# Latents and context laid out with features on partitions by the host; norm factors applied there, without transposes ahead of the projections

## The chip, the cores and the metric

The kernel runs on one core of a Trainium2 chip. The metric is the device time of one execution in microseconds (us); less is better. TensorE (PE in the profile) multiplies matrices; VectorE (DVE), ScalarE (ACT) and GpSimd (POOL) do the elementwise work; SyncE (SP) issues nearly all DMAs. PEld is the load of a matmul's stationary operand.

## The reference, cut to what matters here

One layer of a diffusion backbone: 512 latent tokens and 256 context tokens of 1024 features. The part that the change touches is the first norm, its modulation, and the first two groups of projection columns (384 for the latent queries, 256 for the latent keys and values):

```python
def rms_norm(x, g):
    y = x * lax.rsqrt(jnp.mean(x * x, axis=-1, keepdims=True) + EPS)
    return y * g
...
mod = jax.nn.silu(c) @ w_ada[layer] + b_ada[layer]
sh1, sc1, gt1, sh2, sc2, gt2 = jnp.split(mod[:, None, :], 6, axis=-1)
h  = rms_norm(x_lat, norm1_g) * (1 + sc1) + sh1
hc = rms_norm(x_ctx, norm1_g) * (1 + sc1c) + sh1c
...
q_c, kv_c, ... = split_columns(h @ w_in)
q_cc, kv_cc, ... = split_columns(hc @ w_in)
```

Behind it come latent attention, gated linear attention, a merge of both, and a gated MLP with a 3x3 convolution.

## The kernel before

A product in fp32 accuracy is made of three matmuls in the faster fp32r type: every operand is split into a high part (a cast) and a low part (operand less high part), and `mm3` multiplies high by high, high by low and low by high. The split of weights is a cast on ACT and a subtraction on POOL (`split`); that of the modulated tokens was two DVE instructions.

The features are cut into eight blocks of 128, j = 0 to 7. For each block, the projection loop (lines 553 to 679) needs three things:

- the modulation: the block's columns of `w_ada` (`load_ada`, two tiles of 512 KB) times `silu(c)` and `silu(c_ctx)`. `modulation(j)` makes 16 small matmuls and copies the result to SBUF (`rows`); `factors(j, rows)` turns it by one matmul with `sel` and leaves `shc` (shift) and `scc` (scale times norm gain) of the block, one number for each feature, that is for each partition;
- the block of tokens with features on partitions. The host gives tokens on partitions, so `squared` (sum of squares of a token on ACT), `rstd_exp` (reciprocal root) and `normalised` (DVE, in place) work there, then `columns` turns four 128x128 squares on PE into PSUM, `modulated` scales and shifts them on ACT, and casts and subtracts on DVE;
- the block's weights: `load_w`, `split_latents`.

Then `kv_latents(j)` makes six matmuls of 128x512 and `q_latents(j)` nine, all accumulating in PSUM over the blocks. Step j of the loop does the modulation of block n = j+1, the key-value products of block j, the factors of block n, the query products of block j, and between them starts the tokens of block n. Blocks of the context are turned in j = 5, 6 and 7; their products come behind the loop (`ctx_latents`).

Ahead of the loop, block 0 is done in two halves of 256 tokens: the first needs only the first two tiles of `x`. `fill` issues matmuls whose result is not used; eight stand at the very start, three behind the first factors.

In this stage PE, DVE, ACT, POOL and SP all keep the order in which the code is written (`pinned`), each engine in its own queue; behind the loop more and more of the order is set by a scheduler that works on a model of the time. DMAs count on eight semaphores in turn, so an issue waits for the transfer eight places ahead of it. Tiles come from pools: `raw` (3 buffers, the second half of `w_ada`'s blocks), `kT` (4, the weights), `P` (4, rows and modulated tokens), `s` (30 of 128x1024, most others). `split_wq(0)` splits the first block of `w_uq`, which is used behind the loop.

After the loop `totals` and `spread` serve two more norms: `spread` turns a column of 128 numbers into a 128x128 square with equal columns, by a matmul of the broadcast column with the identity.

Of the kernel before, what the change touches and what calls it, by code (L numbers as in the profile page):

```python
# [18 lines left out]
D = 1024  # L19
# [52 lines left out]
def block_kernel(ctx: ExitStack, tc: tile.TileContext, p, out):  # L72
# [276 lines left out]
    with tc.tile_pool(name="e1", bufs=1) as e1:  # L349
# [29 lines left out]

        def load_wq(k):  # L380
            wq_raw.append(EK())
            SY.dma_start(out=wq_raw[k], in_=w_uq[:, k, :])
# [9 lines left out]
        def split_latents(j, parts=(0, 1)):  # L392
            r = wraw[j]
            if j % 2 == 0 and 0 in parts:
# [3 lines left out]
            for i in parts:  # L398
                (h_, l_), w = both[i]
                if len(parts) == 1 and i == 1:  # L400
                    V.tensor_copy(h_, w)
                    sub(G, l_, w, f(h_))
                else:
                    split(h_, l_, w)
# [4 lines left out]
        def split_wq(k):  # L409
# [63 lines left out]
        def squared(t0):  # L473

            ss = sm(2, "ssx2")
            for t in range(2):
                A.activation(junk, xs[t0 + t], AF.Square, accum_out=ss[:, t:t + 1])
            return ss

        def normalised(t, a, b):  # L480

            V.tensor_scalar(out=xs[t][:, a:b], in0=xs[t][:, a:b], scalar1=rx[t // 2][:, t % 2:t % 2 + 1], scalar2=None,
                            op0=ALU.mult)

        rx = [None, None, None]

# [25 lines left out]
        tps = [0]  # L512

        def columns(j, ctx_, t0, n):

            tps[0] += not ctx_
            tp = (mp if j < 4 else single[j // 2 - 1])[:, j % 2 * 256:j % 2 * 256 + 256] if ctx_ else single[1 + tps[0] % 2]
            for t in range(n):
                PE.transpose(tp[:, t * 128:(t + 1) * 128], xs[4 * ctx_ + t0 + t][:, j * 128:(j + 1) * 128], ident)
            return tp  # L520

        def modulated(j, ctx_, t0, n, tp):
            ht = EP()
            if (j, ctx_, t0) == (0, 0, 0):
                V.tensor_scalar(out=ht[:, 0:128 * n], in0=tp[:, 0:128 * n], scalar1=scc[:, 0, 0:1],
                                scalar2=shc[:, 0, 0:1], op0=ALU.mult, op1=ALU.add)
            else:
# [27 lines left out]
        load_x(0)  # L555
        A.dma_start(out=cst[:, 0:132], in_=p["consts"][:, 0:132])
        load_x(1)
        load_ada(0)
        load_x(2)
        load_w(0, 384, 640)  # L560
        load_x(3)
        load_w(0, 0, 384)
# [3 lines left out]
        fill(accK, 8)  # L566
# [12 lines left out]
        ss = squared(0)  # L579
        rx[0] = rstd_exp(ss, 2, 1.0 / D)  # L580
        for t in range(2):
            normalised(t, 0, 256)
        rows = modulation(0)
        tp = columns(0, 0, 0, 2)
        factors(0, rows)
        fill(accK, 3)
        ss = sm(2, "ssx2")
        A.activation(junk, xs[2], AF.Square, accum_out=ss[:, 0:1])
        modulated(0, 0, 0, 2, tp)
        split_latents(0, [0])  # L590
        split_latents(0, [1])
        A.activation(junk, xs[3], AF.Square, accum_out=ss[:, 1:2])
        kv_latents(0, 0, 256)
        q_latents(0, 0, 256)
        rx[1] = rstd_exp(ss, 2, 1.0 / D)
# [1186 lines left out]
```

## Time and profile before

| | |
|---|---|
| median of 3 runs | 877.91 us (877.88 to 878.12) |
| profiled execution | 878.03 us |
| its span, first to last instruction | 876.3 us |
| granted TensorE clock, mean | 0.999 |
| first projection matmul (block 0, key-value) | 12.71 us |
| factor product of block 2 / 6 | 22.54 / 43.87 us |
| first key-value matmul of block 7 | 53.49 us |
| DMA moved in the span | 130.79 MB |

Times inside an execution count from the span's first instruction. In the rows of the timeline, the first number is the start, the second the length of the group; then the engine, the line (nearly all are L89, the line of the helper that issues every instruction), the operation, what it writes and reads (by tile names, buffer numbers left out), its shape and how many of it stand in the group, and in brackets how long the engine was idle before and what ended that. A matmul in plain fp32 appears as two records; an fp32r matmul and a transpose appear as one. `p` and `pb` are PSUM tiles, `cst` holds the identity.

### The profile page before, as it was taken

Reading aid. Unit: us, or ns where it says so; the run is one execution under the profiler, and the core shown is the slowest. Engines: PE = TensorE matmul, PEld = TensorE weight load, DVE = VectorE, ACT = ScalarE, POOL = GpSimd, SP = SyncE. Lnnn points to the kernel's source line nnn. Section 1 sums busy time; section 2 is a strip of 40 time slices with the busy share of each in tenths; the row PEclk is TensorE's granted clock in tenths of the full one; section 3 lists DMA queues with packets and bytes.
Section 4 is the critical chain, followed back from the end, with each engine's and each line's share of the span. In section 5 each row is a group of like instructions: output and inputs, shape, how many; then the busy total and the mean of one; then the engine's idle time right before and its main releaser. Section 6 shows DMA issues by size and latency. Waiting matters only on the chain.

```text
span 876.3 us, 12667 instructions
## 1 busy us (share of the span) xinstructions
PE 864.8 (99%) x4741; PEld 734.7 (84%) x4741; DVE 641.2 (73%) x1040; ACT 415.7 (47%) x671; POOL 374.6 (43%) x248
## 2 busy tenths in 40 slices
PE   8999999999999999999999999999999999999996
PEld 6888899888888888888888889888888888888885
DVE  6487788875978786985776665777776677677866
ACT  4366676773454545444545324433334334456415
POOL 3302364450534242534561404877767676400004
PEclk9999999999999999999999999999999999999999
DMA  9920001215313342535872512655536656386602
GB/s 357 380 77 1 1 6 32 74 49 193 108 37 132 109 132 61 176 101 210 306 288 85 180 49 73 221 194 206 199 124 231 218 193 194 100 300 221 225 30 97
DMA packets 41360, 130.79 MB, mean 149 GB/s; under 512 B 4785, under 2 KB 5313, under 8 KB 41298
## 3 DMA queue, kind: packets, MB, share of 16 engines
q1 hardware_dynamic: 40098, 126.87, 42.0%
q10 hardware_dynamic: 1008, 2.49, 0.7%
q8 instruction: 37, 0.61, 0.3%
q0 software_dynamic: 192, 0.63, 0.2%
q14 instruction: 25, 0.20, 0.1%
HBM read 116.13 MB, written 13.63 MB: 148 GB/s over the span
## 4 chain that ended last, share of the span: by engine, by line
PE 94%; DVE 3%; ACT 1%; issue 1%; POOL 1%; ACTq 0%; POOLq 0%
PE pb L89 50%; PE p L89 23%; PE pb L88 15%; PE p L88 6%; DVE s L89 1%; DVE mx L89 1%; DVE kT L89 0%; ACT P L89 0%; DVE P L89 0%; ACT s L89 0%; ACT kT L89 0%; POOL wlo L89 0%; DVE X L89 0%; DVE pl L89 0%; POOL s L89 0%
## 5 line engine op out<-in xcount | busy, mean ns | idle before, releaser
L89 POOL TENSOR_TENSOR wlo<-raw,whi 128x1024 fp32r<-128x1024 f32 (+1 forms) x93 | 213.0, 2298 | 254.7 <-ACT whi L89 221.1
L89 PE MATMUL pb<-s,whi 128*128 128x512 f32 (+1 forms) x874 | 269.5, 389 | 0.0
L89 PEld LDWEIGHTS pb<-s,whi 128*128 128x128 f32 x874 | 163.3, 188 | 33.5
L89 ACT CAST whi<-raw 128x1024 fp32r<-128x1024 f32 (+1 forms) x108 | 105.3, 977 | 159.3 <-PE pb L89 75.6
L89 PE MATMUL pb<-s,wlo 128*128 128x512 f32 (+1 forms) x437 | 169.9, 389 | 0.0
L89 DVE SCALAR_TENSOR_TENSOR ac<-pb,cwT,ac 128x441 f32<-128x441 f32 (+2 forms) x160 | 111.0, 694 | 23.4 <-ACT ac L89 18.9
L88 PE MATMUL pb<-s,whi 128*128 128x512 f32 x320 | 101.2, 394 | 0.0
L89 PEld LDWEIGHTS pb<-s,wlo 128*128 128x128 f32 x437 | 82.0, 188 | 17.0
L89 PE MATMUL p<-s,s 128*128 128x512 f32 (+1 forms) x302 | 72.2, 390 | 0.6 <-DVE s L89 0.6
L88 PEld LDWEIGHTS pb<-s,whi 128*128 128x128 f32 x320 | 59.3, 188 | 11.5
L89 PEld LDWEIGHTS p<-s,s 128*128 128x128 f32 x302 | 55.4, 188 | 13.4 <-issue 1.9
L88 PE MATMUL pb<-s,wlo 128*128 128x512 f32 x160 | 62.8, 392 | 0.0
L89 PE MATMUL p<-whi,s 128*128 128x512 f32 x168 | 56.3, 393 | 0.0
L89 PE MATMUL pb<-whi,s 128*128 128x512 f32 x164 | 53.5, 390 | 0.0
L89 POOL TENSOR_TENSOR s<-s,edge 128x512 f32<-128x512 f32 x7 | 10.4, 1503 | 93.7 <-ACT s L89 93.7
L89 PE MATMUL p<-s,whi 128*128 128x256 f32 (+1 forms) x220 | 50.2, 322 | 0.0
L89 PE MATMUL pb<-s,s 128*32 128x128 f32 (+2 forms) x340 | 46.1, 319 | 0.0
L89 DVE TENSOR_TENSOR pl<-pb,ph 128x512 fp32r<-128x512 f32 x48 | 32.9, 686 | 13.3 <-ACT ph L89 12.8
L89 PE MATMUL p<-kT,s 128*128 128x512 f32 (+1 forms) x192 | 41.2, 350 | 0.9 <-ACT P L89 0.9
L89 PEld LDWEIGHTS pb<-s,s 128*128 128x128 f32 (+1 forms) x340 | 36.1, 159 | 5.8 <-issue 0.7
L89 ACT CAST ph<-pb 128x512 fp32r<-128x512 f32 x48 | 28.2, 587 | 20.9 <-PE pb L89 20.8
L89 PEld LDWEIGHTS p<-s,whi 128*128 128x128 f32 x220 | 35.7, 191 | 2.2
(269 smaller groups left out, 1655.6 us busy)
## 6 DMA issues: line engine op xcount, KB each, us to landing
raw<-in_up_dram SPq DMA_DIRECT2D x44, 512.0 KB, 4.2
rawd<-in_w_down_dram SPq DMA_DIRECT2D x22, 512.0 KB, 5.1
ws<-rawd SPq DMA_DIRECT2D x18, 512.0 KB, 5.4
s<-in_ada_rest_dram SPq DMA_DIRECT2D x12, 512.0 KB, 5.4
xn<-in_ada_rest_dram SPq DMA_DIRECT2D x10, 512.0 KB, 4.6
s<-in_ada_first_dram SPq DMA_DIRECT2D x8, 512.0 KB, 9.0
raw<-in_ada_first_dram SPq DMA_DIRECT2D x8, 512.0 KB, 8.1
raw<-in_in_ga_dram SPq DMA_DIRECT2D x8, 512.0 KB, 3.5
```

The source lines that it names most:

```text
L88: return fn(*args, **kw)
L89: ins = fn(*args, **kw)
```

## The change

The host adds `x_t`, the latents with features on partitions (four tiles, each with two blocks of 512 tokens), and `ctx_t` (two tiles, each with four blocks of 256). The kernel loads `x_t` in place of `x` at the start, and `ctx_t` besides `ctx`.

- The sums of squares of the latents: ACT squares three tiles and half of the fourth, DVE the other half; DVE adds the two blocks of a tile; `norm_sums` adds over partitions by matmuls with a column of ones, 16 in all. `spread_norm` turns the four columns of reciprocal roots into a 128x512 tile in PSUM, `spread_[0]`, by four transposes of a broadcast column. It stays there for all blocks.
- `modulated_in` replaces `columns`, `normalised` and `modulated`: `scaled_` (DVE) multiplies the block by `scc` and by the spread factors, `high` (ACT) adds the shift and rounds to the high part, `low` (DVE) adds the shift and subtracts the high part. `tiles` issues these three stages for several blocks side by side.
- The context keeps its squares on tokens (`x`'s layout, on ACT at j = 2); its spread factors follow at j = 4, and its blocks are modulated at j = 4 to 7.
- Block 0's queries are done over 512 tokens at once; its key-value products keep two halves. Modulation 7 is issued one step earlier.
- `fill` is 5 at the start and then single ones of 128 columns.
- `split_wq(0)` comes at j = 5 in place of 6, with its subtractions on POOL. `spread` uses transposes. In the merge loop (line 1386) a part of the gate moves from j = 6 to j = 5.

```diff
+        def load_xt(i):
+            xT[i] = S4f()
+            SY.dma_start(out=xT[i], in_=p["x_t"][i])
...
-                sub(V, l3[:, :, a:b], r3[:, :, c:c + b - a], f(h3[:, :, a:b]))
+                sub(V if k else G, l3[:, :, a:b], r3[:, :, c:c + b - a], f(h3[:, :, a:b]))
...
-        def columns(j, ctx_, t0, n):
-
-            tps[0] += not ctx_
-            tp = (mp if j < 4 else single[j // 2 - 1])[:, j % 2 * 256:j % 2 * 256 + 256] if ctx_ else single[1 + tps[0] % 2]
+        spread_ = [single[1], single[2]]
+
+        def spread_norm(dst, r_, n):
+
             for t in range(n):
-                PE.transpose(tp[:, t * 128:(t + 1) * 128], xs[4 * ctx_ + t0 + t][:, j * 128:(j + 1) * 128], ident)
-            return tp
-
-        def modulated(j, ctx_, t0, n, tp):
-            ht = EP()
...
-                A.activation(ht[:, 0:128 * n], tp[:, 0:128 * n], AF.Identity, scale=scc[:, j, ctx_:ctx_ + 1],
-                             bias=shc[:, j, ctx_:ctx_ + 1])
-            h_, l_ = cxt(j) if ctx_ else lat(j, t0 * 128, n * 128)
-            V.tensor_copy(h_, ht[:, 0:128 * n])
-            sub(V, l_, ht[:, 0:128 * n], f(h_))
+                PE.transpose(dst[:, t * 128:t * 128 + 128], r_[:, t:t + 1].broadcast_to([128, 128]), ident)
+
+        def norm_sums(sq, first, last):
+
+            for t in range(4):
+                mm(single[2][:, t:t + 1], sq[:, t * 128:t * 128 + 128], ones[:, 0:1], first and t == 0, last and t == 3)
+
+        def modulated_in(j, ctx_, a=0, b=512):
+            b = (b, 256)[ctx_]
+            ht = EP()[:, 0:b - a]
+            x_ = cT[j // 4][:, j % 4 * 256:j % 4 * 256 + 256] if ctx_ else xT[j // 2][:, j % 2 * 512 + a:j % 2 * 512 + b]
+            shift = shc[:, j, ctx_:ctx_ + 1]
+            h_, l_ = (cxt if ctx_ else lat)(j, a, b - a)
+
+            def scaled_():
+                V.scalar_tensor_tensor(out=ht, in0=x_, scalar=scc[:, j, ctx_:ctx_ + 1], in1=spread_[ctx_][:, a:b],
+                                       op0=ALU.mult, op1=ALU.mult)
+
+            def high():
+                A.activation(h_, ht, AF.Identity, bias=shift)
+
+            def low():
+                V.scalar_tensor_tensor(out=l_, in0=ht, scalar=shift, in1=f(h_), op0=ALU.add, op1=ALU.subtract)
...
-        load_x(0)
+        for i in range(4):
+            load_xt(i)
...
-        fill(accK, 8)
+        fill(accK, 5)
...
+        a_, b_ = slice(0, 512), slice(512, 1024)
+        for i in range(4):
+            sq = S4f()
+            if i < 3:
+                A.activation(sq, xT[i], AF.Square)
+            else:
+                A.activation(sq[:, a_], xT[i][:, a_], AF.Square)
+                tt(V, sq[:, b_], xT[i][:, b_], xT[i][:, b_], ALU.mult)
+            tt(V, sq[:, a_], sq[:, a_], sq[:, b_], ALU.add)
+            norm_sums(sq, i == 0, i == 3)
+            if i < 2:
+                fill(accK, 1, 128)
+        rx = rstd_exp(single[2][:, 0:4], 4, 1.0 / D)
         rows = modulation(0)
-        tp = columns(0, 0, 0, 2)
         factors(0, rows)
-        fill(accK, 3)
...
+        fill(accK, 1, 128)
+        spread_norm(spread_[0], rx, 4)
+        fill(accK, 1, 128)
+        split_latents(0)
+        tiles((0, 0, 0, 256), (0, 0, 256, 512))
         kv_latents(0, 0, 256)
-        q_latents(0, 0, 256)
...
+        kv_latents(0, 256, 512)
+        q_latents(0, 0, 512, 0, 1)
         rows = modulation(1)
...
             if n < 8:
                 split_latents(n)
-                factors(n, rows)
+                if n < 7:
+                    factors(n, rows)
+                if n == 6:
+                    rows = modulation(7)
                 q_latents(j, 0, 512, 0, 2)
-                modulated(n, 0, 0, 4, tp)
-                if j >= 5:
-                    context(2 * j - 10, 2 * j - 8)
+                if j == 4:
+                    spread_norm(spread_[1], rx, 2)
+                tiles((n, 0), *[(2 * j - 8 + i, 1) for i in range(2) if j >= 4])
                 q_latents(j, 0, 512, 2, 3)
             extra_loads(j)
...
-            elif j == 6:
+            if j == 5:
                 split_wq(0)
...
-                mm(ps[:, t * 128:(t + 1) * 128], r_[:, t:t + 1].broadcast_to([128, 128]), ident)
+                PE.transpose(ps[:, t * 128:(t + 1) * 128], r_[:, t:t + 1].broadcast_to([128, 128]), ident)
...
-            if j == 6:
+            if j == 5:
                 m_, gh, gl = mp_tile(), *[tl(em_, [128, 1024], F32R, "xn", 3) for _ in range(2)]
```

Outside this stage each engine's instructions stand in the order of before, but for the moved part of the gate. Three places where the order changes:

PE around the first loads and products, now: `s_21` is the constant tile of the fills, `s_50` to `s_53` are the squares, `raw` and `s_42` the block of `w_ada`, `rr` the reciprocal roots, `s_11` and `s_15` the high and low part of the tokens, `s_25` the key-value weights.

```order
L89 MATMUL p_32_110<-s_21_93 128x256 x5
L89 MATMUL pb_114<-ones_74,s_50_154 128x1 x4
L89 MATMUL p_32_110<-s_21_93 128x128
L89 MATMUL pb_114<-ones_74,s_51_162 128x1 x4
L89 MATMUL p_32_110<-s_21_93 128x128
L89 MATMUL pb_114<-ones_74,s_52_170 128x1 x4
L89 MATMUL pb_114<-ones_74,s_53_177 128x1 x4
L89 MATMUL pb_115<-s_42_126,s_21_93 32x128 x8
L89 MATMUL p_32_110<-s_21_93 128x128
L89 MATMUL pb_115<-raw_127,s_21_93 32x128 x8
L89 MATMUL pb_115<-cst_71,P_211 128x4
```

The 16 sums over all four tiles of `x_t` now stand ahead of the first modulation, where before only fills were.

DVE at block 6 of the tokens, before: `pb_115` holds the modulation, `s_84` and `s_85` are the context on tokens, `s_14` and `s_18` the high and low part of block 6, `s_96` and `s_97` those of the context.

```order
L89 COPY P_585<-pb_115 128x128
L89 TENSOR_SCALAR s_84_420<-s_84_420,rr_108_556 128x512
L89 TENSOR_SCALAR s_85_422<-s_85_422,rr_108_556 128x512
L89 TENSOR_SCALAR shc_108<-pb_115,pcol_72 128x2
L89 TENSOR_SCALAR scc_109<-pb_115,b1sc_81,pcol_72 128x2
L89 CAST s_14_86<-P_610 128x512
L89 TENSOR_TENSOR s_18_90<-P_610,s_14_86 128x512
```

And now, where `pb_113` and `pb_114` hold the spread factors, `s_41` and `s_85` the features of latents and context, and `s_101` the context's low part:

```order
L89 COPY P_569<-pb_115 128x128
L89 TENSOR_SCALAR shc_108<-pb_115,pcol_72 128x2
L89 TENSOR_SCALAR scc_109<-pb_115,b1sc_81,pcol_72 128x2
L89 COPY P_602<-pb_115 128x128
L89 SCALAR_TENSOR_TENSOR P_610<-s_41_123,scc_109,pb_113 128x512
L89 SCALAR_TENSOR_TENSOR P_611<-s_85_406,scc_109,pb_114 128x256
L89 SCALAR_TENSOR_TENSOR P_612<-s_85_406,scc_109,pb_114 128x256
L89 SCALAR_TENSOR_TENSOR s_18_90<-P_610,shc_108,s_14_86 128x512
L89 SCALAR_TENSOR_TENSOR s_101_481<-P_611,shc_108,s_100_480 128x256
L89 SCALAR_TENSOR_TENSOR s_101_481<-P_612,shc_108,s_100_480 128x256
```

The copy of modulation 7's rows and two context tiles now stand between the factors of block 6 and its low part.

POOL at the end of the loop, now: `kT_463` and `kT_469` are the weights of blocks 6 and 7, `kT_538` the first block of `w_uq`. Before, its two rows were not on POOL.

```order
L89 TENSOR_TENSOR s_28_106<-kT_463,s_27_105 128x256
L89 TENSOR_TENSOR wlo_578<-kT_463,whi_577 128x384
L89 TENSOR_TENSOR wlo_626<-kT_538,whi_625 128x8x96
L89 TENSOR_TENSOR wlo_626<-kT_538,whi_625 128x8x32
L89 TENSOR_TENSOR s_28_106<-kT_469,s_27_105 128x256
L89 TENSOR_TENSOR wlo_578<-kT_469,whi_577 128x384
```

The low part of `w_uq` now stands ahead of that of the weights of block 7.

More of the change, by code (lines that the diff above doesn't have):

```diff
@@ L378, in load_x, with load_ct @@
             SY.dma_start(out=xs[t], in_=src)
+        xT, cT = {}, {}
+        def load_xt(i):
+            xT[i] = S4f()
+            SY.dma_start(out=xT[i], in_=p["x_t"][i])
+        def load_ct(i):
+            cT[i] = S4f()
+            SY.dma_start(out=cT[i], in_=p["ctx_t"][i])
         def load_wq(k):
@@ L390, in block_kernel, with split_latents @@
         wpair = []
-        def split_latents(j, parts=(0, 1)):
+        def split_latents(j):
             r = wraw[j]
-            if j % 2 == 0 and 0 in parts:
+            if j % 2 == 0:
                 wpair[:] = whl()
@@ L397, in split_latents @@
             both = (([kvw[j // 4][i][:, j % 4, :] for i in range(2)], r[:, 384:640]), (wj[j], r[:, 0:384]))
[L398 to L404, printed above, removed]
+            for (h_, l_), w in both:
+                split(h_, l_, w)
         wqh, wql = [], []
@@ new lines, in norm_sums @@
+        def norm_sums(sq, first, last):
[14 more added lines that the diff above has]
+                V.scalar_tensor_tensor(out=l_, in0=ht, scalar=shift, in1=f(h_), op0=ALU.add, op1=ALU.subtract)
+            return scaled_, high, low
@@ L534, in kv_w, with tiles @@
+        def tiles(*of):
+            for step_ in zip(*[modulated_in(*of_) for of_ in of]):
+                for x in step_:
+                    x()
         def kv_w(j, k):
@@ L578, in block_kernel @@
                             op0=ALU.add)
[L579 to L582, printed above, removed]
+        a_, b_ = slice(0, 512), slice(512, 1024)
[11 more added lines that the diff above has]
+        rx = rstd_exp(single[2][:, 0:4], 4, 1.0 / D)
         rows = modulation(0)
-        tp = columns(0, 0, 0, 2)
         factors(0, rows)
-        fill(accK, 3)
[L587 to L592, printed above, removed]
-        kv_latents(0, 0, 256)
-        q_latents(0, 0, 256)
-        rx[1] = rstd_exp(ss, 2, 1.0 / D)
-        for t in (2, 3):
-            normalised(t, 0, 256)
-        for t in (0, 1):
-            normalised(t, 256, 1024)
-        tp = columns(0, 0, 2, 2)
-        modulated(0, 0, 2, 2, tp)
+        fill(accK, 1, 128)
[3 more added lines that the diff above has]
+        tiles((0, 0, 0, 256), (0, 0, 256, 512))
+        kv_latents(0, 0, 256)
+        kv_latents(0, 256, 512)
+        q_latents(0, 0, 512, 0, 1)
         rows = modulation(1)
-        tp = columns(1, 0, 0, 4)
-        kv_latents(0, 256, 512)
-        normalised(2, 256, 1024)
+        q_latents(0, 0, 512, 1, 2)
         factors(1, rows)
-        normalised(3, 256, 1024)
         split_latents(1)
-        modulated(1, 0, 0, 4, tp)
-        q_latents(0, 256, 512)
-        load_ada(2)
-        load_w(2)
-        load_ada(3)
-        load_w(3)
+        tiles((1, 0))
+        q_latents(0, 0, 512, 2, 3)
+        for j in (2, 3):
+            load_ada(j)
+            load_w(j)
         def extra_loads(j):
@@ L641, in extra_loads @@
                     load_wkv(k)
-        def context(a, b):
-            tp = [columns(kt, 1, 0, 2) for kt in range(a, b)]
-            for kt in range(a, b):
-                modulated(kt, 1, 0, 2, tp[kt - a])
         mraw_, ssc = [], sm(2, "ssx2")
@@ L650, in block_kernel @@
             n = j + 1
-            if n < 8:
-                tp = columns(n, 0, 0, 4)
+            if n < 7:
                 rows = modulation(n)
-            if j in (5, 6):
-                for t in (4, 5):
-                    normalised(t, 512 * (j - 5), 512 * (j - 4))
-            elif j == 7:
-                context(4, 8)
+            elif n == 7:
+                factors(n, rows)
+            else:
+                tiles((6, 1), (7, 1))
             kv_latents(j, 0, 512)
@@ L1762, in _laid_out @@
     rows = [np.asarray(inputs[n]).reshape(-1, 128) for n, _ in ROWS] + [np.asarray(inputs["conv_w"]).reshape(-1, 128)]
+    a["x_t"] = a["x"][0].T.reshape(4, 2, 128, 512).transpose(0, 2, 1, 3).reshape(4, 128, 1024)
+    a["ctx_t"] = a["ctx"][0].T.reshape(2, 4, 128, 256).transpose(0, 2, 1, 3).reshape(2, 128, 1024)
     a["cols"] = np.concatenate(rows, 0).T
```

38 lines of the change are left out of this document (12 added, 26 removed).

## The prediction, made before the changed kernel was timed

> **What bounds the kernel now.** I read the page first (busy shares and the chain that ended last), then the waits of PE, then PE's timeline from 0 to 100 us, where the change lies.
>
> ```profile
> PE 864.8 (99%) x4741; PEld 734.7 (84%) x4741; DVE 641.2 (73%) x1040; ACT 415.7 (47%) x671; POOL 374.6 (43%) x248
> PE 94%; DVE 3%; ACT 1%; issue 1%; POOL 1%; ACTq 0%; POOLq 0%
> PE p L89 <- DVE s L89: 2.6, 2, 2.1
> PE p L89 <- ACT P L89: 0.9, 3, 0.4
> ```
>
> TensorE is busy 99% of the span and makes 94% of the chain; its two longest waits are for DVE, 2.6 us together, 2.1 of them before the very first matmul. So a microsecond taken off PE's queue comes off the span, wherever the other engines still deliver in time. One step of the projection loop, n=4, as PE ran it (start, length, engine, line, operation, count):
>
> ```profile
> 27.88 0.28 PE L89 MATMUL pb<-cst,P 128*128 128x4 f32 x2
> 28.02 0.71 PE L89 MATMUL p<-s,whi 128*128 128x512 f32 x2
> 30.17 0.60 PE L89 MATMUL pb<-cst,s 128*128 128x128 f32 x4
> 30.71 0.64 PE L89 MATMUL pb<-s,s 128*32 128x128 f32 x16
> 31.72 1.66 PE L89 MATMUL p<-s,s 128*128 128x512 f32 x6
> 33.22 0.28 PE L89 MATMUL pb<-cst,P 128*128 128x4 f32 x2
> ```
>
> From the factor product (27.88) to the next (33.22) are 5.34 us: 0.14 for it, 2.15 for the nine query products, 0.54 for four transposes (30.17 to 30.71), 1.01 for the modulation, 1.50 for the six key-value products (0.233 us for each 128x512).
>
> **1. The transposes in the loop.** Nothing on PE's path takes their place, so a step falls to 4.80 us if its operands come in time. What is late next is the chain of the following block: factor product, `scc`, `scaled_` (DVE), `high` (ACT), `low` (DVE), then the block's second key-value product.
>
> ```profile
> 28.34 0.27 DVE L89 TENSOR_SCALAR scc<-pb,b1sc,pcol 128x2 f32<-128x2 f32 x1
> 63.27 0.74 DVE L89 SCALAR_TENSOR_TENSOR s<-p,pcol,s 128x512 fp32r<-128x512 f32 x1
> 66.17 1.13 ACT L89 CAST s<-P 128x512 fp32r<-128x512 f32 x2
> 35.33 0.69 DVE L89 TENSOR_TENSOR s<-P,s 128x512 fp32r<-128x512 f32 x1
> ```
>
> `scc` ends 0.73 after the factor product's start. The trace has no three-operand DVE instruction on just these tiles; the nearest is the row at 63.27, 0.74. The Identity with a bias from one buffer to another isn't there either; it lies between 0.57 (the cast at 66.17, half of 1.13) and the 0.78 that the old Identity takes; I take 0.68. The low part I take as the old subtraction, 0.69. Sum: 0.73+0.74+0.68+0.69 = 2.84. PE's work ahead of that product is 0.14+2.15+1.01+0.23 = 3.53, so 0.7 us is left and the transposes' 0.54 is earned in full at the plain steps.
>
> Three plain steps (n = 3, 4, 5) give 3 x 0.54 = **-1.6 us**. Step 6 has two spreading transposes for the context, 0.3: **-0.25**. The rest of the loop, from the factor product of block 6 to the first key-value product of block 7:
>
> ```profile
> 22.54 0.28 PE L89 MATMUL pb<-cst,P 128*128 128x4 f32 x2
> 43.87 0.28 PE L89 MATMUL pb<-cst,P 128*128 128x4 f32 x2
> 53.49 1.64 PE L89 MATMUL p<-s,s 128*128 128x512 f32 x6
> ```
>
> Before: 53.49 - 43.87 = 9.62, with eight latent and sixteen context transposes. After: 0.14+1.01+2.15+0.14+1.50+2.15 = 7.1, and 0.3 for a wait that is new: DVE now copies the rows of modulation 7 ahead of `scaled_` of block 6 and has two context tiles between `scaled_` and `low` (0.44 each), so `low` comes about 0.3 late. **-2.2 us.**
>
> **2. The start.** Before, only the first 256 tokens were needed for the first product. Now the sums run over features, so all four transfers of `x_t` must land, and a longer chain follows.
>
> ```profile
> 2.06 6.32 PE L89 MATMUL p<-s 128*128 128x256 f32 x16 [2.06 <-DVE s L89]
> 7.49 0.17 DVE L89 TENSOR_SCALAR rv<-ssx 128x2 f32<-128x2 f32 x1 [1.20 <-ACT ph L89]
> 7.58 0.33 SPq L89 DMA_DIRECT2D kT<-in_w_in_dram  x1
> 8.56 0.16 DVE L89 SCALAR_TENSOR_TENSOR rr<-rt,rr 128x2 f32<-128x2 f32 x1
> 8.86 0.33 SPq L89 DMA_DIRECT2D s<-in_ada_first_dram  x1
> 10.01 0.29 DVE L89 COPY P<-pb 128x128 f32<-128x128 f32 x1 [0.64 <-PE pb L89]
> 10.16 1.06 ACT L89 ACTIVATE ph<-s 128x1024 bf16<-128x1024 f32 x1 [2.03 <-DMA s<-in_x_dram]
> 10.60 1.54 PE L89 MATMUL p<-s 128*128 128x256 f32 x6
> 10.91 0.27 DVE L89 TENSOR_SCALAR scc<-pb,b1sc,pcol 128x2 f32<-128x2 f32 x1
> 12.71 1.22 PE L89 MATMUL p<-s,s 128*128 128x256 f32 x6 [0.56 <-DVE s L89]
> 57.02 1.87 PE L89 MATMUL pb<-ones,kT 128*128 128x1 f32 x16
> 75.07 0.88 DVE L89 SCALAR_TENSOR_TENSOR P<-pb,pcol,P 128x256 f32<-128x256 f32 x2
> ```
>
> SP issues once the transfer eight places ahead has landed, so 7.58 and 8.86 are the landings of the two halves of `ada_first` 0, one every 1.28 us, and 10.16 that of the third tile of `x`. In the new order these places hold the third and fourth tile of `x_t` and the first half of `ada_first` 0. The fourth tile lands at 8.9. DVE is then busy with the third add (8.65 to 9.35), squares its half (0.69) and adds (0.66): 10.7. Four sums, half the 57.02 row, to 11.65. The reciprocal root takes 1.23 (7.49 to 8.72): 12.9. Row copy to `scc`, 1.17 (10.01 to 11.18): 14.1, while PE spreads until 14.45. Then `scaled_` 0.44, `high` 0.45, `low` 0.44: 15.85 for the first low product, against 12.71 before. From there PE: key-value products until 17.2, a third of the queries 17.9, modulation 18.9, a third 19.6, factor product, and the 2.84 chain: 22.5 for the second product of block 1. Its five left end at **23.7, the factor product of block 2, against 22.54: +1.2 us.** With work beside it the bounds are 0 (the waits hide each other) and +3.
>
> **3. The last block.** `split_wq(0)` comes a step earlier, and its two subtractions leave DVE for POOL, ahead of those of block 7.
>
> ```profile
> 29.87 0.74 POOL L89 TENSOR_TENSOR s<-kT,s 128x256 fp32r<-128x256 f32 x1 [3.18 <-ACT s L89]
> 29.99 1.16 DVE L89 TENSOR_TENSOR s<-P,s 128x512 fp32r<-128x512 f32 x1
> 30.56 1.45 POOL L89 TENSOR_TENSOR wlo<-kT,whi 128x384 fp32r<-128x384 f32 x1
> 74.45 2.55 POOL L89 TENSOR_TENSOR wlo<-raw,whi 128x512 fp32r<-128x512 f32 x2 [25.14 <-ACT whi L89]
> ```
>
> POOL needs 0.74 for 256 columns and 1.28 for 512, so about 1.9 for 768: 2.65 in all. ACT reaches these casts near 47.0, POOL works on them from 47.8 to 50.4, then on the key-value weights of block 7 (0.75) until 51.2, later where DVE is in its way. PE wants that tile at 50.9. DVE's `low` of block 7 stands at the same time: the subtraction at 29.99 took 1.16 where the one at 35.33 took 0.69, POOL being at work beside the first. I take **+1.0 us**, bounds 0.3 and 2. The Trainium skill, "SBUF — State Buffer", section "Who interferes with whom", says that a DVE instruction with two SBUF inputs and a POOL instruction that reads SBUF exclude each other, the first to start holding the port to its end. By that rule the new `scaled_`, with one input in PSUM, is free, and `low` and the weights queue up behind each other for all of 2.65 us; the sum would be 0.5 us worse. The two rows agree with it in sign, 0.47 us.
>
> **4. Spreading by transposes later.** Four there and then six.
>
> ```profile
> 61.59 0.97 PEld L89 LDWEIGHTS pb<-cst,rr 128*128 128x128 f32 x8
> 62.48 4.79 PEld L89 LDWEIGHTS pb<-s,s 128*128 128x128 f32 x33
> 72.56 1.53 PEld L89 LDWEIGHTS pb<-cst,rr 128*128 128x128 f32 x12
> 74.02 0.30 PEld L89 LDWEIGHTS p<-s,whi 128*128 128x128 f32 x2
> ```
>
> They took 0.89 and 1.46 with no wait shown; as transposes 4 and 6 x 0.135 (30.17 to 30.71): 0.54 and 0.81. **-1.0 us.**
>
> **5. What I cost at nothing.** The loads: `ctx` comes in a second layout, 1.05 MB more in a stream that is full until about 40 us.
>
> ```profile
> GB/s 0 139 373 416 412 415 396 396 407 410 404 395 419 393 410 402 405 383 405 407 397 395 403 406 414 395 370 324 218 178 299 322 52 292 25 5 11 0 0 0
> ```
>
> At 405 GB/s that is 2.6 us. Summing these slices (1.5 us each), block 7 of `ada_first` lands near 42 and the first tile of `w_uq` near 43; they are wanted near 43.3 and 47.0, so some 1 us covers it, and past that it costs microsecond for microsecond. The norm factor of the context and its squares sit on ACT and DVE between steps. The gate's part moved from j=6 to j=5 is work of ACT and DVE in the merge loop, where PE shows no wait; nothing, at most 0.3 either way.
>
> **Sum.** -1.6-0.25-2.2+1.2+1.0-1.0 = -2.85 on a span of 876.3, so 873.45. The profiled execution took 878.03, 1.73 beside its span, and the median of the runs is 877.91: 877.91-2.85 = 875.1.
>
> **Rivals.**
> A, *small gain*: the chain of part 1 becomes the bound. For it speaks that 0.47 us are lost when POOL runs beside `low`; against it that POOL's splits now start after `high`, so `low` gets in first. If a step loses its 0.54, or start and last block cost their upper ends, 2 us of the gain go: 877.1.
> B, *full gain*: the start loses nothing and POOL delivers in time: -2.85-1.2-0.8 = -4.85: 873.1. Against it stands the chain of part 2, which is serial.
> C, *slower, a cold array*. Eight fills took 6.32 us from 2.06, 0.79 each; three from 10.60 took 1.54, 0.51 each, so PE ran slower at first, though the granted clock of the profile is 0.999. The new start has five fills and gaps of about 0.5 us between the sums. If PE stays slow until some 6 us of dense work have passed, its products between 10.7 and about 21 (five of the microseconds there are array work that would double) cost +5: 880.1. It decides from about 2.9 us of doubled work, which is slow until 18. The Trainium skill, "TensorE: Matmul & The Clock Gate", section "What's actually happening", has the array at half rate until a window of about 3.4 us has been busy; by it C hangs on whether sums and fills count as busy. The first rows agree with the half rate.
> D, *loads late*: the second layout pushes block 7 past its time by up to 2.6 us less 1: +1.6, 876.7. Against it: the modulation of block 7 was ready well ahead before.
>
> **How the numbers follow.** Forecast 0.52, A 0.18, B 0.13, C 0.08, D 0.09. Predicted is the forecast, 875.1. B lies at 873.1 and the upper ends of A and D near 878; the range 872.8 to 878.0 leaves out C and the outer ends. A measurement of this kernel tells 0.2% from no change, 1.76 us. Faster by that means below 876.15: most of the forecast and B, a little of A, 0.66. Slower, above 879.67: C, 0.08. The rest, 0.26, is the same.
>
> **What would show it.** In the new profile: the factor product of block 2 near 23.7; 4.8 us between the following ones; a wait of PE for POOL at the key-value products of block 7, near 51; the spreads at 0.54 and 0.81. Wrong would make it: steps above 5.1 us (A), first key-value products of 256 columns at twice the 0.117 that half of a 512 product gives (C), PE waiting for a DMA near 40 (D), or another length between 80 us and the end.

## The result, and the profile after

The changed kernel takes **885.30 us** (median of 4 runs, 882.67 to 887.02), the kernel before in the same session 877.94 (877.88 to 878.12): ratio 1.0079, 95% interval 1.0066 to 1.0093. It is slower by 7.4 us, and its runs scatter over 4.4 us where those of the kernel before scatter over 0.24. The forecast was 875.1, the range ended at 878.0. The profiled execution took 887.02, with a span of 885.2, 8.9 above the 876.3 of before.

The page after: busy time, chain, and the waits of PE (us in total, times, longest):

```profile
PE 871.4 (98%) x4708; PEld 738.3 (83%) x4708; DVE 646.2 (73%) x1025; ACT 414.6 (47%) x667; POOL 380.5 (43%) x250
PE 87%; DVE 6%; ACT 3%; DMA 2%; issue 1%; POOL 1%; SPq 0%; POOLq 0%; ACTq 0%
PE p L89 <- DVE s L89: 3.1, 4, 2.1
PE p L89 <- ACT s L89: 0.9, 2, 0.7
PE pb L89 <- DVE scc L89: 0.5, 1, 0.5
```

PE issues 33 matmuls fewer (4741 to 4708) and is yet busy 6.6 us longer. So the loss is not in waits, which grew by some 2 us; the same matmuls became slower. PE's timeline after shows where:

```profile
2.06 4.64 PE L89 MATMUL p<-s 128*128 128x256 f32 x10 [2.06 <-DVE s L89]
6.77 1.87 PE L89 MATMUL pb<-ones,s 128*128 128x1 f32 x8
11.20 3.41 PE L89 MATMUL pb<-ones,s 128*128 128x1 f32 x16
14.54 1.08 PE L89 MATMUL pb<-s,s 128*32 128x128 f32 x16
18.78 1.06 PE L89 MATMUL pb<-cst,rr 128*128 128x128 f32 x4
20.96 3.24 PE L89 MATMUL p<-s,s 128*128 128x256 f32 x12 [0.69 <-ACT s L89]
25.36 0.64 PE L89 MATMUL pb<-s,s 128*32 128x128 f32 x16
31.56 0.28 PE L89 MATMUL pb<-cst,P 128*128 128x4 f32 x2
36.42 0.28 PE L89 MATMUL pb<-cst,P 128*128 128x4 f32 x2
41.30 0.28 PE L89 MATMUL pb<-cst,P 128*128 128x4 f32 x2
51.52 0.36 PE L89 MATMUL pb<-cst,P 128*128 128x4 f32 x2
59.45 0.39 PE L89 MATMUL p<-s,s 128*128 128x512 f32 x1
60.05 1.79 PE L89 MATMUL p<-s,s 128*128 128x512 f32 x5 [0.21 <-DVE s L89]
65.97 4.61 PE L89 MATMUL pb<-s,s 128*128 128x256 f32 x24
81.62 0.71 PE L89 MATMUL p<-s,whi 128*128 128x512 f32 x2
```

The context products before:

```profile
58.75 3.11 PE L89 MATMUL pb<-s,s 128*128 128x256 f32 x24
```

The sixteen matmuls of a modulation take 1.08 us at 14.54 and 0.64 at 25.36; the 24 context products at 65.97 took 3.11 before and 4.61 now. Half the sums alone (x16 from 11.20) take 3.41. In the stretches from 62.80 and from 66.21 (PE, PEld, DVE, ACT, POOL busy, granted clock, DMA share, GB/s) the profile names the reason:

```profile
62.80:66.21 3.41, 3.31 (x23) 2.69 (x22) 1.81 (x4) 2.69 (x6) 0.00 (x0) 1.00 0.02 5
66.21:69.62 3.41, 3.41 (x18) 3.41 (x18) 2.61 (x8) 2.71 (x7) 0.00 (x0) 0.50 0.01 2
```

From 66.21 to 69.62 PE ran at half rate, though in the 3.41 us ahead of that it was busy for 3.31. By the trace's record of the granted clock, full rate first came at 25.25 us; before, it came at 7.34 and stayed until PE's last matmul had ended. The profiled execution is the longest of the four. In the two shortest the mean granted clock is lower, 0.990 and 0.989 against 0.996, though they took 4.4 and 2.4 us less. That mean counts lost rate only behind the first recorded change, so they had full rate early and lost it again: by the mean, some 18 to 19 us at half rate with the end of the run, an estimate.

Where the 8.9 us lie, from the starts of the same instructions in the two profiled executions:

| stretch on PE | before | after | difference |
|---|---|---|---|
| start, to the factor product of block 2 | 22.54 | 31.56 | +9.02 |
| from there to the key-value products of block 7 | 30.95 | 27.89 | -3.06 |
| those six products | 1.48 | 2.23 | +0.75 |
| to the first context product behind the totals | 3.78 | 4.29 | +0.51 |
| context products of that piece | 2.95 | 4.45 | +1.50 |
| two spreadings (0.81 and 1.25 before; 0.35 and 0.58 after) | 2.06 | 0.93 | -1.13 |
| first keys, 84 to 88 us before | | | +0.46 |
| merge loop, near 490 us | | | +0.79 |

They sum to 8.84. The loop gave three quarters of what it should and the spreadings a little more than theirs, 4.19 together; the start alone took back more than twice that.

### The profile page after: what moved, and what is told of

Its sections match the earlier page's. It is cut to its first block, busy times and chain, and to the rows that moved or that the text cites. A ratio compares the mean times of both kernels' runs of the same rounds, so it can differ in the third digit from the quotient of the medians.

```text
span 885.2 us, 12573 instructions
## 1 busy us (share of the span) xinstructions
PE 871.4 (98%) x4708; PEld 738.3 (83%) x4708; DVE 646.2 (73%) x1025; ACT 414.6 (47%) x667; POOL 380.5 (43%) x250
## 4 chain that ended last, share of the span: by engine, by line
PE 87%; DVE 6%; ACT 3%; DMA 2%; issue 1%; POOL 1%; SPq 0%; POOLq 0%; ACTq 0%
PE pb L89 45%; PE p L89 21%; PE pb L88 14%; PE p L88 6%; DVE s L89 2%; ACT s L89 1%; DVE P L89 1%; DMA wa<-in_ada_rest_dram 1%; DVE gt L89 1%; DMA xn<-in_ada_rest_dram 1%; DVE mx L89 1%; DVE sg L89 0%; DMA pcol<-in_cols_dram 0%; POOL wlo L89 0%; DVE kT L89 0%
## 5 line engine op out<-in xcount | busy, mean ns | idle before, releaser
L89 POOL TENSOR_TENSOR wlo<-raw,whi 128x1024 fp32r<-128x1024 f32 (+1 forms) x93 | 216.1, 2331 | 245.4 <-ACT whi L89 212.4
L89 PE MATMUL pb<-s,whi 128*128 128x512 f32 x872 | 269.3, 390 | 0.0
L89 PE MATMUL pb<-s,wlo 128*128 128x512 f32 x436 | 169.7, 389 | 0.0
L88 PE MATMUL pb<-s,whi 128*128 128x512 f32 x320 | 101.3, 394 | 0.0
L89 PE MATMUL p<-s,s 128*128 128x512 f32 (+1 forms) x302 | 74.3, 397 | 2.0 <-DVE s L89 1.0
L88 PE MATMUL pb<-s,wlo 128*128 128x512 f32 x160 | 62.8, 392 | 0.0
L89 PE MATMUL pb<-s,s 128*32 128x128 f32 (+2 forms) x340 | 48.2, 332 | 0.5 <-DVE scc L89 0.5
L89 ACT ACTIVATE ac<-ac 128x512 f32<-128x512 f32 x22 | 13.9, 632 | 52.1 <-DVE ac L89 52.0
```

The source lines that it names most:

```text
L88: return fn(*args, **kw)
L89: ins = fn(*args, **kw)
```

## The experiments

All compare with runs of the kernel before on the same chip in the same session. Until the ninth I write "T-clock" for the theory that matmuls with one output column do not keep the array at full rate.

**1 to 4: what keeps the rate.** The first widens the sums:

```diff
-                mm(single[2][:, t:t + 1], sq[:, t * 128:t * 128 + 128], ones[:, 0:1], first and t == 0, last and t == 3)
+                mm(single[2][:, t * 128:t * 128 + 128], sq[:, t * 128:t * 128 + 128], ones.broadcast_to([128, 128]), first and t == 0, last and t == 3)
```

> The sums of squares of the latents are taken with 128 columns of ones in place of one; as many matmuls, the same value in each column, of which one is read. Theory T-clock (matmuls with one column leave the array at half rate, and it stayed there until 25.25 us): with 128 columns the sums stream, the full rate comes between 8 and 13 us, the twelve first projections of keys take 1.6 to 1.8 us in place of 3.24 and begin near 17, the factor product of block 2 stands near 25, and the time is 878.8 us (877.5 to 881), about 6 under the changed kernel. Rival T-chain (the start is late because all four transposed x tiles must have landed and the chain behind them is serial, whatever the rate): sums cost as much or more, the first projection of keys stays near 21, factor product near 31.5, time 885 or more.

The second changes `fill(accK, 5)` of the changed kernel to `fill(accK, 8)`, the third does both, the fourth changes the 8 of the kernel before to 5.

> Eight dense matmuls at the start in place of five, as the kernel before had; sums with one column stay. Theory T-clock: eight of 0.85 us at half rate are 6.8 us, which holds a whole stretch of 3.4 us wherever the stretches lie, so full rate by 9 us; whether it then lasts through the sums (no streaming for some 3 us) is open: 878 us if it lasts, 884 to 886 if half rate is back in the sums. Rival T-fills (it was the number of dense matmuls at the start alone): 878 us and a steady full rate. Rival T-chain: no change, 885 us, with the sums half as long and the first projection of keys still near 20.

> Both: eight dense matmuls and sums with 128 columns. T-clock: full rate by 9 us and kept through the sums, first projection of keys at 16 to 17, factor product of block 2 at 24 to 25, 877.5 us (876.5 to 879), and the runs lie within 0.5 us of each other. T-fills: no less than eight dense matmuls alone. T-chain: 885 us.

> The kernel before with five dense matmuls at the start in place of eight, nothing else. T-clock: five of 0.85 us are 4.3 us, which need not hold a whole stretch of 3.4 us; the transposes of the latents then run at half rate for some us, and the time is 879 to 883 us, with runs that differ by over 1 us; or 878 where the stretches lie well or the transposes count as streaming. T-chain: 878 us.

| | median us (runs from, to) | ratio to before, 95% |
|---|---|---|
| before | 878.15 (877.51 to 878.93) | |
| 1, wide sums | 879.83 (878.18 to 881.24) | 1.0014 (1.0005 to 1.0022) |
| 2, eight dense | 883.26 (880.71 to 885.68) | 1.0061 (1.0047 to 1.0076) |
| 3, both | 879.77 (878.99 to 882.01) | 1.0023 (1.0014 to 1.0031) |
| 4, before with five dense | 878.33 (877.67 to 878.97) | 1.0002 (0.9993 to 1.0011) |

PE's timeline of the first:

```profile
10.66 1.16 PE L89 MATMUL pb<-ones,s 128*128 128x128 f32 x8 [0.24 <-DVE s L89]
16.13 2.10 PE L89 MATMUL p<-s,s 128*128 128x256 f32 x12 [0.89 <-ACT s L89]
25.03 0.28 PE L89 MATMUL pb<-cst,P 128*128 128x4 f32 x2
59.45 4.62 PE L89 MATMUL pb<-s,s 128*128 128x256 f32 x24
```

A hundred and twenty-eight times the columns, and the sums cost less: eight matmul records in 1.16 us, at full rate, where one column took 1.71 to 1.87 at half rate. Full rate came at 5.60 us, still among the five fills, and the sums kept it. The twelve products take 2.10 in place of 3.24 (1.6 to 1.8 was expected), and block 2 stands at 25.03 in place of 31.56. That is T-clock's picture; T-chain, with 885, falls. The totals still cost the 24 context products their 1.5 us here (59.45). The second shows how the rate is lost, in the stretches of its profile:

```profile
8.68:12.09 3.41, 3.18 (x40) 2.94 (x39) 1.92 (x4) 0.79 (x2) 0.00 (x0) 1.00 1.03 407
12.09:22.33 10.24, 9.14 (x59) 7.08 (x55) 3.48 (x10) 2.53 (x8) 3.39 (x4) 0.50 1.03 406
```

Eight dense matmuls had brought full rate by 5.27 us; the stretch of sums, busy 3.18 of 3.41 us, lost it again, and it came back only at 22.33. So the fills alone are not it, as the fourth also says: with five of them the kernel before loses nothing measurable. The 879 to 883 that T-clock gave the fourth did not come, but the 878 that it allowed besides; which of the matmuls behind the fills hold the rate there is not shown. The second and the third differ in the width of the sums alone: the third kept full rate from 7.66 us to PE's last matmul in its profile. Its median is still 2.3 above the expected 877.5, and its runs scatter over 3 us, against the expected 0.5; the three shortest (878.99 to 879.08) have a mean granted clock of 0.999, the other eight 0.994 to 0.997, so most of them lost a stretch somewhere.

**5 to 8: the rest, on top of the third.** The fifth gives the totals 128 and 64 columns in the same way. The sixth adds `if j == 6` for the gate's part, as before the change. The seventh takes the fifth and puts `split_wq(0)` back:

```diff
-                sub(V if k else G, l3[:, :, a:b], r3[:, :, c:c + b - a], f(h3[:, :, a:b]))
+                sub(V, l3[:, :, a:b], r3[:, :, c:c + b - a], f(h3[:, :, a:b]))
...
-            if j == 5:
+            if j == 6:
                 split_wq(0)
```

The eighth joins both, has five fills, and spreads ahead of `factors(0, rows)`.

> The third experiment's kernel, and the totals of the keys' and queries' norms also taken with many columns of ones (128 for the first, 64 for the second) in place of one. T-clock: the stretch at half rate that came in the totals, worth 1.6 us, comes no more; the runs close up to within 0.7 us at 878.9 us (878.5 to 879.3), 0.9 under the third experiment's median, and full rate lasts from under 9 us to the end. Rival (that stretch has another cause, such as a load on the chip, or follows 41 us after the first change of rate by a timer): it stays in most of the runs, which spread from 879 to 882 as before, median 879.8.

> The fifth experiment's kernel, with the gate's part of the merge loop back at j = 6, where the kernel before had it. If the 0.8 us that the changed kernel loses between 420 us and the end come from that move (a transfer of the gate's weights that lands late holds DVE, then ACT, then the cast of the next weights, then PE): 0.8 us less than the fifth, and TensorE busy for 100.00 of the 100 us from 400 to 500. Rival (the loss comes from the later arrival of PE at that loop, or chance): the same as the fifth.

> The fifth experiment's kernel, with split_wq(0) back at j = 6 and its subtractions back on DVE. If POOL's two subtractions (2.57 us for the 768 columns) slow the three low parts of block 7 on DVE beside them (3.27 us there, 1.54 for those of block 6), then those take 1.6 us again, PE no longer waits in the key-value products of block 7, and 0.7 us go. Rival (DVE is late for other reasons, its copy of the rows of modulation 7 and the two context tiles; or PE then waits for the query weights): the same as the fifth, within 0.2.

> All of it, on the changed kernel: sums and totals with many columns, the gate's part at j = 6, split_wq(0) at j = 6 on DVE, five dense matmuls at the start, and the transposes that spread the norm factors ahead of the factor product of block 0. By the terms as measured: 878.9 for the fifth, -0.8 gate, -0.7 split, -0.7 for five dense matmuls in place of eight, -0.4 for the spreading a step earlier: 876.3 us (875.6 to 877.3), 1.9 under the kernel before. If terms overlap at the start: 877.

| | median us (runs from, to) | ratio to before, 95% |
|---|---|---|
| before | 877.90 (877.48 to 878.36) | |
| 5, wide totals | 878.69 (878.48 to 880.36) | 1.0012 (1.0004 to 1.0021) |
| 6, gate back | 879.03 (878.55 to 880.47) | 1.0015 (1.0006 to 1.0023) |
| 7, split back | 878.68 (878.25 to 879.76) | 1.0009 (1.0000 to 1.0018) |
| 8, all | 878.80 (878.16 to 881.07) | 1.0015 (1.0007 to 1.0024) |

The fifth does as expected: ten of eleven runs within 0.7 us, the median 1.1 under the third's, where 0.9 was expected. The sixth gains nothing, and its TensorE is busy 100.00 of the 100 us from 400 to 500, but so it is in the third, fifth and seventh, which have the moved gate. In the changed kernel's profile the merge loop lost its 0.79 where DVE waited for a transfer:

```profile
467.84 1.54 DVE L89 SCALAR_TENSOR_TENSOR gt<-wa,csilu,gt 128x256 f32<-128x256 f32 x1 [0.61 <-DMA wa<-in_ada_rest_dram]
```

and PE then waited 0.50 for DVE at 487. By the starts of the same instructions, such a loss is in two of the six profiles up to here with the moved gate (the changed kernel's and the first's, 0.72) and in neither of the two with the gate back; what makes it occur is not settled.

The profile of the sixth shows another way to lose the rate, in the gap ahead of the first products:

```profile
14.00:17.40 3.40, 1.89 (x16) 1.42 (x12) 2.38 (x8) 1.13 (x4) 1.25 (x2) 1.00 1.03 405
17.43:20.84 3.41, 3.41 (x14) 3.06 (x14) 0.27 (x1) 0.46 (x2) 1.70 (x2) 0.50 1.03 400
```

The eighth has the same stretch (17.62 to 21.03); spreading earlier only widened the gap ahead of its first products, 1.23 us where the fifth has 0.89, and they start no earlier (16.77 and 16.59). Its 876.3 was missed by 2.5, and the lost stretch isn't the reason: six of its runs, with the higher mean clocks of 0.997 and 0.998, took 878.16 to 878.80. The gate's 0.8 and the split's 0.7 in its sum are not there in the sixth and the seventh either.

The seventh answers the last block. DVE's low parts of block 7 (three instructions, then the first of them alone), POOL beside them, and PE's third to sixth product, in the changed kernel:

```profile
55.33 1.54 DVE L89 SCALAR_TENSOR_TENSOR s<-P,shc,s 128x512 fp32r<-128x512 f32 x3
58.77 3.25 DVE L89 SCALAR_TENSOR_TENSOR s<-P,shc,s 128x512 fp32r<-128x512 f32 x3
58.77 1.22 DVE L89 SCALAR_TENSOR_TENSOR s<-P,shc,s 128x512 fp32r<-128x512 f32 x1
56.89 2.55 POOL L89 TENSOR_TENSOR wlo<-kT,whi 128x768 fp32r<-128x768 f32 x2 [4.79 <-ACT whi L89]
59.40 1.18 POOL L89 TENSOR_TENSOR s<-kT,s 128x256 fp32r<-128x256 f32 x1
60.64 1.20 PE L89 MATMUL p<-s,s 128*128 128x512 f32 x4
```

and in the seventh (DVE, then PE):

```profile
53.07 1.54 DVE L89 SCALAR_TENSOR_TENSOR s<-P,shc,s 128x512 fp32r<-128x512 f32 x3
53.78 1.54 PE L89 MATMUL p<-s,s 128*128 128x512 f32 x6
57.75 2.31 PE L89 MATMUL pb<-ones,kT 128*128 128x128 f32 x16 [0.39 <-ACT kT L89]
```

The low parts of block 6 (55.33) take 1.54, the same three of block 7 take 3.25 while POOL subtracts, and 1.54 again without it. In the changed kernel PE's second product starts at 60.05, as the first low part ends (60.00), and its third at 60.64, as POOL's low part of the key-value weights ends (60.58): two holds, one for DVE and one for POOL. In the seventh both are gone; from the first product to the first query product it is 1.38 us, where the fifth has 2.20. But 0.39 of it turns into a wait for ACT's squares ahead of the totals, and the median does not move: the expected 0.7 was not there to be had.

**9: narrow sums, with dense matmuls between.** On the second experiment: `fill(accK, 2)` behind the sums of each of the first three tiles.

> The changed kernel with eight dense matmuls at the start and two dense ones of 256 columns behind the sums of each of the first three tiles; the sums keep their one column. It tells what about the sums costs the rate. If it is that the array streams too little (T-clock), the dense matmuls in between hold the full rate as the wide sums did: full rate from 5 to 8 us on and none lost before 20 us, and about 880 us (878.5 to 881.5; a stretch may still be lost in the totals). Rival (matmuls with one column drive the rate down by themselves, whatever runs between): half rate again from about 12 us, 883 us, as with eight dense matmuls alone.

880.59 us (879.84 to 884.00; before 878.01), ratio 1.0036 (1.0023 to 1.0049). In PE's timeline:

```profile
13.12 0.95 PE L89 MATMUL pb<-ones,s 128*128 128x1 f32 x8
18.39 2.10 PE L89 MATMUL p<-s,s 128*128 128x256 f32 x12 [0.89 <-ACT s L89]
```

Full rate in its profile from 6.63 us to PE's last matmul, with sums of one column: they do not drive the rate down, they only fail to hold it by themselves. The fills put the sums 1.5 us later, hence a time above the third's.

**10: one part alone.** In the kernel before, `spread` with `PE.transpose` in place of `mm`.

> The kernel before with one part of the change alone: the two later spreadings of norm factors by transposes in place of matmuls. The prediction's step 4 has -1.0 us. Rival: PE's time goes, but DVE, which serves the first keys some 12 us later, was only just ahead; it becomes the later of the two there and 0.4 to 0.5 come back, so -0.6.

877.31 us (877.04 to 878.01; before 878.01), ratio 0.9992 (0.9983 to 1.0001). The spreadings take 0.35 and 0.58, -1.13 as in the changed kernel; by the starts of the same instructions, 0.45 of it is lost again at the first keys, where DVE's parts of them come last. What was left, -0.7, is near the rival's -0.6; by the times alone it can't be told from none, and the trace decides.

**11: a shorter start.** On the seventh, with the gate at j = 6: the fourth tile's sums are taken of both halves without DVE's addition, two small fills go, two wider ones stand ahead of the first products.

> The seventh experiment's kernel with a shorter chain at the start and with the gate's part at j = 6. The sums of the fourth tile of x_t are taken of both halves of its squares, without DVE's addition of the halves (0.66 us on the chain); the two small dense matmuls inside the modulation of block 0 and ahead of the spreading are gone (0.5 us), and two of 256 columns fill the gap ahead of the first key-value products. If the start is a serial chain at full rate, about 1.2 us go: first key-value products at 15.7 where the seventh had 16.93, no lost stretch near 17 us, and 877.4 us (876.8 to 878.3), 0.5 under the kernel before. Rival (the chain at the start hangs on modulation 0 and its loads, not on the sums): 878.6, as the seventh.

878.57 us (878.07 to 879.56; before 878.01), ratio 1.0006 (0.9998 to 1.0015): the rival's value. PE, DVE and POOL in its timeline:

```profile
9.91 2.84 PE L89 MATMUL pb<-ones,s 128*128 128x128 f32 x24
16.82 2.09 PE L89 MATMUL p<-s,s 128*128 128x256 f32 x12 [0.27 <-ACT s L89]
13.66 0.16 DVE L89 TENSOR_TENSOR rt<-rt,rv 128x4 f32<-128x4 f32 x1
13.86 0.69 DVE L89 SCALAR_TENSOR_TENSOR rr<-rt,rr 128x4 f32<-128x4 f32 x1
13.81 0.72 POOL L89 TENSOR_TENSOR s<-kT,s 128x256 fp32r<-128x256 f32 x1 [7.01 <-ACT s L89]
```

No stretch was lost, but the extra sums now fill PE from 9.91 to 12.75, so the chain is no shorter. And its last link, four columns wide, takes 0.69 beside POOL where its neighbour takes 0.16; so it does in the changed kernel.

**12 to 14: the loop without the start.** The kernel before, with the later spreads by transposes and, from block 4 (twelfth) or block 2 (thirteenth) on, `modulated_in` on the transposed layout, with four transposes that spread the norm factors:

```diff
+                if n < 2:
                     tp = columns(n, 0, 0, 4)
+                elif n == 2:
+                    for t in range(4):
+                        PE.transpose(single[1][:, t * 128:t * 128 + 128],
+                                     rx[t // 2][:, t % 2:t % 2 + 1].broadcast_to([128, 128]), ident)
```

The fourteenth is the thirteenth with `single[2]` in place of `mp` for the context's first four transposed blocks.

> The kernel before with its own start; only blocks 4 to 7 of the latents come from the transposed layout, with the norm factors spread by four transposes at block 4, and the later spreads are transposes as in the tenth. The start, the context and split_wq are as before; 1.05 MB more is loaded, as in the changed kernel. By the prediction's part 1 three steps lose 0.54 each and the fourth gives its transposes for the spreading ones: -1.6, and with the tenth's -0.7 in all 875.7 us (875.2 to 876.5). Rival (a step's gain hangs on the new start, or DVE, which must still normalise and transpose the context, becomes the bound): 877 or more. Rival (the loads come late by 2.6 us and TensorE waits for a DMA near 45): 877 to 878.

> As the twelfth, with blocks 2 to 7 from the transposed layout: 1.57 MB more loads than the kernel before, 3.9 us of the stream at 405 GB/s. If the loads still come in time, two more steps of 0.54: 874.6 us. Rival (the stream that is full until 40 us can't take it, and block 7 of the modulation's weights is late): 875.7 or more, with TensorE waiting for a DMA.

> The thirteenth experiment's kernel with the first four transposed context blocks in another PSUM bank than the one that modulation uses. In the thirteenth TensorE waited 1.09 us ahead of modulation 7 for ACT, which reads the context's transposes from that bank, in its order behind the new high part of block 6. If it is the shared bank: that wait goes, 1.0 us less than the thirteenth, 876.1 us (875.6 to 876.6), 0.24% under the kernel before. Rival (DVE, which brings the high and low parts of block 6 and the context's, is next): half of it comes back at block 7, 876.6.

Measured: the twelfth 878.82 us (877.90 to 878.90; before 878.21), ratio 1.0004 (0.9995 to 1.0013); the thirteenth 877.11 (876.62 to 879.54; same before), 0.9989 (0.9981 to 0.9998); the fourteenth 877.46 (877.00 to 878.18; before 878.31), 0.9991 (0.9982 to 1.0000). The thirteenth on PE, then the fourteenth at the place of its last row:

```profile
22.49 0.28 PE L89 MATMUL pb<-cst,P 128*128 128x4 f32 x2
27.37 0.28 PE L89 MATMUL pb<-cst,P 128*128 128x4 f32 x2
46.74 0.65 PE L89 MATMUL pb<-s,s 128*32 128x128 f32 x16 [1.09 <-ACT P L89]
```

```profile
49.83 0.38 PE L89 MATMUL pb<-cst,P 128*128 128x4 f32 x2 [1.20 <-DVE P L89]
```

The twelfth missed its 875.7 by 3.1, and the rival with DVE as the bound fits in part: one step takes 4.89 (33.61 to 38.50), the next 5.42 with 0.38 of wait for DVE. The thirteenth missed its 874.6 by 2.5, and not by its rival's cause, since PE waits for no DMA. A step is 4.88 us there with the old start as well (22.49 to 27.37). Ahead of modulation 7, though, in both PE waits 1.09 for ACT: the bank that modulation writes still holds transposes of the context, and ACT reads them behind the new high part. In another bank that wait is gone, and one of 1.20 for DVE stands at the next factor product: DVE's copy of the rows of modulation 7 is queued behind the context's high and low parts. The expected 876.1 was missed by 1.4. The thirteenth is the one version of fourteen whose interval lies below the kernel before, by 0.11% (0.02 to 0.19), a margin that so many trials make less sure. In its profile 0.43 of the gain is the loop (30.52 from the factor product of block 2 to block 7, where 30.95 stood); the spreadings of the tenth give the most of it.

## Why the prediction was wrong, by its steps

**Part 2, the start, is the step that failed**, with rival C. The sum took every length at the start as on a warm array (four sums from the 57.02 row, half of 1.87) and gave the start +1.2, bounds 0 and +3; the loss of the rate had no term, only rival C, at 0.08. C came true and was larger: it makes +6.2 of the factor product of block 2, its 5 on top of the 1.2, and measured is +9.0. Its sign was there, products of 256 columns at 0.25 us each (twelve from 20.96 to 24.00), twice the 0.117. C left open whether the sums count as busy, and had the slow products end at about 21. The sums counted for too little: the array was at half rate until 25.25 us, which made the sums themselves, modulation 0, the spreading and the first products twice as long. Experiments 1, 3 and 9 take that away in two ways. C also looked at the start alone: the totals cost 1.5 us more by the same mechanism.

At full rate the start is still +2.5 (25.03 less 22.54 in the first experiment) to +3.2 (third). Of the missing 1.3, 0.53 is the last link of the reciprocal root (0.69 in place of 0.16), which I had taken from the kernel before, where nothing ran beside it. So with five fills the bounds held for the chain, with eight they just did not, and the value held in neither.

**Part 1, the loop, held in kind and gave three quarters of its size**: -3.06 where -4.05 stood. The first two steps take 4.86 and 4.88 us against 4.80 (5.34 before), the third 4.99, the fourth gains 0.11 in place of 0.25. From the factor product of block 6 to block 7 it is 7.93 (51.52 to 59.45) against 7.4, with 0.5 of wait for DVE's `scc` ahead of modulation 7 where I had put 0.3 of wait later. (The eight latent transposes that the prediction counts in that stretch are four, those of block 7; its sum does not use the number.)

**Part 3, the last block, held in kind and nearly in size.** PE waits once for DVE's first low part, which takes 1.22 beside POOL, and once for POOL's key-value weights, some 0.36 us each: +0.75 for the +1.0 I took. Another +0.51 ahead of the totals has no term in the sum. Taking POOL's part away (seventh) gave 0.82 at one place and lost 0.39 at the next.
The Trainium skill, "SBUF — State Buffer", section "Who interferes with whom", has two such instructions exclude each other; the rows agree, 3.25 us beside POOL and 1.54 without, though the 0.5 that the prediction had worked out by it on top did not come.

**Part 4, the spreads, held** (-1.13 for -1.0), in part by luck: start to start they took 2.06 before where I read 2.35 from the loads of operands, and 0.93 after where I put 1.35. And 0.46 of it came back at the first keys, which I did not look for.

**Part 5.** The loads cost nothing that a trace shows. The gate's move went with +0.79 in this execution, +0.72 in the first experiment's, and nothing in four others; "at most 0.3" was wrong for the two.

**Rivals.** B's condition, a start that loses nothing, did not occur, nor did D: PE waits for no DMA in the loop. A's chain cost half a microsecond, not 2. With wide sums, wide totals and eight fills, so that the rate lasts, the changed kernel still comes to 878.7 (fifth, seventh), 0.8 above the kernel before; with five fills the eighth's six runs with the higher mean clock take 878.16 to 878.80, also above. So without C the forecast of a gain was wrong too. In the third experiment's profile, at full rate and with a span of 877.2, the terms miss mine by +2.0 at the start (3.2 for 1.2; 0.7 of it with the three more fills, by the first experiment's 25.03), +1.0 in the loop, +0.5 ahead of the totals, +0.46 at the keys, -0.24 in the last block and -0.13 at the spreads: 3.6 in all, which turns -2.85 into +0.75; the span is 0.9 longer.

The Trainium skill, "TensorE: Matmul & The Clock Gate", section "What's actually happening", says that a window of about 3.4 us of activity releases the array and that the window runs freely. The traces agree: every change of rate here lies a multiple of 3.41 us from the others of its run (25.25, 66.21, 69.62 in the changed kernel), and kernels with the same eight fills got full rate at 5.27 (second), 7.34 (before) and 7.66 us (third). What counts as activity decided this case, and the second experiment's stretch, busy 3.18 us of 3.41 and lost, shows that it isn't the busy time of the profile.

## What to carry to other kernels

A kernel whose bound is PE has its rate as a resource of its own: work that replaces matmuls by waits or by matmuls of one column near the start, or between two dense stages, may slow what follows: here by 1.5 us behind 2.07 us of totals. Give sums over partitions many columns where that costs little (1.16 us for 128 columns against 0.95 for one, both at full rate). And a gain on PE's queue is worth what the next engine in line leaves of it: here 0.46 of 1.13 and 0.39 of 0.82 were lost again at its next meeting with DVE or ACT.

## What the runs showed of the hardware

- Busy time on PE is not what holds the rate: 3.18 and 3.31 us busy in stretches of 3.41, mostly matmuls with one column, were followed by half rate. A stretch of the first experiment with products for about 1.3 of 3.41 us beside its totals lost it, one of the kernel before with about 1.9 (55.12 to 57.02, up to 58.53) did not; the point between lies somewhere there, an estimate from these two. Busy time would put it elsewhere: the sixth experiment's stretch was busy for 1.89 us, the eighth's for 2.04, and both lost it.
- The profile's granted clock shows 1.00 until the first change that the trace records: 25.3 us at half rate in the changed kernel do not lower the mean, 0.996. The lengths of known groups (0.64 or 1.08 for a modulation) are the surer sign.
- Where such stretches fall varies from run to run, so that a kernel near the edge scatters: 4.4 us in the changed kernel, 0.7 in ten of eleven runs of the fifth.
- A DVE instruction on 128x4 numbers took 0.69 us in place of 0.16 when a POOL subtraction of 0.72 had started 0.05 ahead of it.
